# Encoder block on one core: last branch-B unit interleaved differently with the gate products, own staging pool for gate copies, token sums in halves, meta columns on VectorE

## The chip, the cores and the metric

The kernel runs on one core of a Trainium2 chip. Its engines are TensorE (PE; weight loads are listed as PEld), VectorE (DVE), ScalarE (ACT), GpSimd (POOL) and SyncE (SP), each with its own in-order queue. SP only starts transfers; ACT can start them too, on a queue of its own. The metric is the device time of one execution in microseconds (us).

## What is computed

One encoder block of width 1024 over 1024 tokens and 16 meta tokens, in float32. Two attention branches run on the same normed input, each with its gate, and a SwiGLU feed-forward network follows.

```python
def diff_attn_rows(q1, q2, k1, k2, v, qpos, kpos, key_real, slopes, lam):
    ...
    s1 = jnp.einsum('bqhd,bkhd->bhqk', q1, k1).astype(jnp.float32) * scale + bias
    s2 = jnp.einsum('bqhd,bkhd->bhqk', q2, k2).astype(jnp.float32) * scale + bias
    attn = jax.nn.softmax(s1, axis=-1) - lam * jax.nn.softmax(s2, axis=-1)
    return jnp.einsum('bhqk,bkhe->bqhe', attn.astype(v.dtype), v)

def mixer_block(h, w_in, ...):
    proj = h @ w_in
    ...
    y_a = differential_attention(...)
    y_b = windowed_gqa(...)
    merged = jax.nn.sigmoid(ga) * (y_a @ w_ba) + jax.nn.sigmoid(gb) * (y_b @ w_bb)
    return merged @ w_o

h = h + mixer_block(rms_norm(h, norm_mix[layer]), w_in[layer], ...)
h = h + swiglu(rms_norm(h, norm_ffn[layer]), w_ff_gate[layer], w_ff_up[layer], w_ff_down[layer])
return rms_norm(h, norm_final)[:, N_META:]
```

## The kernel before, in words

Float32 products are made of split operands: a high part and a low remainder, each product of two such operands taking three matmuls. The stages follow one another: norm and transposes, projections, branch B, branch A together with the gate projections, the merge of the branches (ppa), the output projection (po), and the feed-forward network (pg at L1699, pd at L1803). This change touches the end of branch B and branch A.

Branch B has 16 units (group g, token tile t), made by `attend_b`. A unit makes scores, an exp and a scaling; its `finish` then transposes each block on PE (T; L453, L439 for the meta block bmd), splits the result on ACT and DVE into btr (btm for the meta block), and multiplies by the values (V; L450, L459) into bpy. For the last unit (1,7) the steps are named T0, V0 for the meta block, T1, V1 for block 6 and T2, V2 for block 7 in this text; the code's list `last_unit` has them in that order, and in the change's table "V0" is the meta block's V, "T1" block 6 and so on. The unit's sum by1 is built by an ACT copy and a DVE add (L462) and stored to yb_d (L464).

Branch A has 32 tiles (head h, token tile t). In a tile `scores_a` makes two score maps m = 1 and m = 0 (aps, L1035), each with a 704-wide DVE operation (L1038) and a 336-wide one (L1042, which reads a copied distance strip far_m made by POOL at L982), an exp on ACT (L1046), and then the combination of the two maps on DVE (L1052) into as0_0 or as0_1 by turns. A meta copy (L1053) repeats 2 x 16 meta columns behind the combined map. Transposes (L1064), products with the values (L1077) and a norm follow. The psum bank pair "two" that the 704-wide operation reads has a single buffer.

The gate projections are computed by a scheme of products of block sums; `order_g` lists pairs (k, p), here called quarters. One quarter is 12 matmuls (pg, L928) on the split normed input hT_hi, hT_lo and an operand wopg that POOL makes from weights (cast L830, difference L831, sums L811 and L812) loaded by SP (L790). Results leave through ACT or DVE to staging tiles (L934, L948, L959, L964, L966) and are stored by SP (`flush_stores`, L892). `turn_into` (L860) loads sums of token halves t_d over parts of hT.

The order on PE is written out by hand: the strings SLOTS say for each tile which piece comes next, s scores, g four gate products, t transposes, n later steps. The order on POOL is written out at the head of branch A only. On the other engines a scheduler sets the order from its simulated times; `queue_behind` and `issue_after` are the places where the program sets an order between two instructions. Tiles of pools that share an address wait for the earlier user.

## Time and profile before

| what | value |
|---|---|
| median of three runs | 1423.49 us (1421.62 to 1425.19) |
| profiled execution | 1422.3 us, of which span 1420.5 us |
| mean granted TensorE clock | 0.997 |
| branch A begins (first aps) | at 280.49 us |
| last value product of branch A begins | at 596.46 us |

In the profile a row of the timeline gives the start, the duration, the engine, the line, the operation with output and inputs, how many stand in a row, and in brackets how long the engine stood idle before and what ended that. "Granted clock" is the share of full speed at which PE was let run. A row of the waits has the waiting group, what it waited for, and the total, the count and the longest wait.

### The profile page before, as it was taken

To read this page: it belongs to the slowest core of one execution; us is meant where nothing else is said; L and a number is where in the kernel's file an instruction comes from. 1 tells how busy PE (TensorE), PEld (TensorE's weight loads), DVE (VectorE), ACT (ScalarE), POOL (GpSimd) and SP (SyncE) were. 2 spreads that over 40 slices of the span, in tenths; PEclk is the share of its full clock that TensorE was granted. 3 is DMA by queue.
4 is the path that set the end of the run, shared out by engine and by line. 5 is a ranking of instruction groups with operands and counts; after the bars stand their busy time and mean duration, and the time that the engine had idled before them with its cause. 6 is when DMAs were issued, how large, how long until landed. Compare 5 with 4: busy or idle time off the path is not lost.

```text
span 1420.5 us, 20697 instructions
## 1 busy us (share of the span) xinstructions
PE 1400.6 (99%) x7171; PEld 1201.6 (85%) x7171; DVE 920.5 (65%) x1587; ACT 674.6 (47%) x1285; POOL 657.9 (46%) x666
## 2 busy tenths in 40 slices
PE   9999999899999999999999999999999999999998
PEld 8989999778888888878888888888888888888886
DVE  6546666656677777666978956544544453787566
ACT  6356565534444555555346644333333333444454
POOL 4156884366777767622503054554444441000442
PEclk9999999999999999999999999999999999999999
DMA  8446658543796453296422724432233223954333
GB/s 233 92 124 187 190 176 295 150 158 104 258 336 208 142 187 120 82 332 202 148 104 90 207 91 147 149 106 98 100 112 104 97 97 108 361 184 144 121 127 142
DMA packets 192952, 227.73 MB, mean 160 GB/s; under 512 B 16888, under 2 KB 126400, under 8 KB 192720
## 3 DMA queue, kind: packets, MB, share of 16 engines
q1 hardware_dynamic: 190656, 223.46, 48.3%
q10 hardware_dynamic: 2192, 2.96, 0.7%
q8 instruction: 56, 0.92, 0.3%
q14 instruction: 48, 0.39, 0.1%
HBM read 152.48 MB, written 68.39 MB: 155 GB/s over the span
## 4 chain that ended last, share of the span: by engine, by line
PE 73%; DVE 2%; POOL 1%; DMA 1%; issue 1%; ACT 1%; SPq 0%; DVEq 0%; POOLq 0%; ACTq 0%
PE pg L1699 29%; PE pd L1803 15%; PE pg L928 8%; PE ppa L746 6%; PE po L1602 4%; PE aps L1035 3%; PE apy L1077 3%; PE apt L1064 2%; PE po L1610 2%; DVE as L1052 1%; ACT as L1046 1%; POOL wopg L831 1%; DMA g_d<-g 1%; PE ptn_f L1567 0%; DVE as L1038 0%
## 5 line engine op out<-in xcount | busy, mean ns | idle before, releaser
L1699 PE MATMUL pg<-t,wop 128*128 128x512 f32 x1056 | 242.4, 389 | 0.0
L1699 PEld LDWEIGHTS pg<-t,wop 128*128 128x128 f32 x1056 | 198.2, 188 | 41.2
L121 POOL TENSOR_TENSOR wop<-wf,wop 128x512 fp32r<-128x512 f32 x114 | 150.7, 1323 | 164.3 <-ACT wop L120 152.5
L1803 PE MATMUL pd<-ob,oa 128*128 128x512 f32 x924 | 209.6, 389 | 0.0
L1803 PEld LDWEIGHTS pd<-ob,oa 128*128 128x128 f32 x924 | 173.4, 188 | 36.0
L928 PE MATMUL pg<-hT_hi,wopg 128*128 128x512 f32 x488 | 185.2, 405 | 7.0 <-ACT p L934 2.1
L1699 PE MATMUL pg<-b,wop 128*128 128x512 f32 x792 | 183.3, 389 | 0.0
L1699 PEld LDWEIGHTS pg<-b,wop 128*128 128x128 f32 x792 | 148.4, 188 | 30.7
L1046 ACT ACTIVATE as<-as,amn 128x1040 f32<-128x1040 f32 x64 | 74.7, 1166 | 97.7 <-DVE amn L1042 96.2
L120 ACT ACTIVATE wop<-wf 128x512 fp32r<-128x512 f32 x128 | 80.8, 632 | 72.3 <-PE pg L1699 50.9
L928 PEld LDWEIGHTS pg<-hT_hi,wopg 128*128 128x128 f32 x488 | 92.4, 190 | 24.6 <-POOL wopg L831 3.5
L121 POOL TENSOR_TENSOR oa<-ra,oa 128x512 fp32r<-128x512 f32 x27 | 34.9, 1294 | 168.6 <-ACT oa L120 167.2
L120 ACT ACTIVATE oa<-ra 128x512 fp32r<-128x512 f32 x77 | 48.7, 632 | 108.5 <-PE pd L1803 50.1
L928 PE MATMUL pg<-hT_lo,wopg 128*128 128x512 f32 x244 | 96.5, 396 | 0.0
L1035 PE MATMUL aps<-ak,aq 128*128 128x352 f32 (+1 forms) x384 | 87.5, 336 | 1.2 <-DVE amn L1038 1.2
L1476 DVE TENSOR_TENSOR s<-wf,wf 128x512 f32<-128x512 f32 x22 | 15.6, 709 | 111.6 <-DMA wf<-in_w_ff_up_dram 71.6
L1038 DVE CUSTOM_DVE_ANT_0 as<-aps,dist,far_a 128x704 f32<-128x704 f32 x64 | 60.4, 944 | 24.7 <-PE aps L1035 24.5
L1035 PEld LDWEIGHTS aps<-ak,aq 128*128 128x128 f32 x384 | 64.2, 191 | 9.8 <-DVE amn L1038 3.2
L414 DVE CUSTOM_DVE_ANT_0 bs<-bps,tbx,nsink 128x432 f32<-128x432 f32 (+1 forms) x64 | 38.5, 628 | 45.6 <-PE bps L412 31.8
L424 POOL TENSOR_SCALAR bs<-bs,bdn 128x432 f32<-128x432 f32 (+1 forms) x64 | 36.9, 597 | 51.1 <-DVE bdn L422 31.7
L1067 ACT ACTIVATE at<-apt 128x512 fp32r<-128x512 f32 (+1 forms) x96 | 46.3, 487 | 25.8 <-PE apt L1064 25.5
L1726 ACT COPY p<-pg 128x512 f32<-128x512 f32 x44 | 25.8, 587 | 66.6 <-PE pg L1699 66.6
(340 smaller groups left out, 3144.5 us busy)
## 6 DMA issues: line engine op xcount, KB each, us to landing
ra<-aop SPq DMA_DIRECT2D x77, 256.0 KB, 2.6
wf<-in_w_ff_gate_dram SPq DMA_DIRECT2D x25, 512.0 KB, 3.6
wf<-in_w_ff_up_dram SPq DMA_DIRECT2D x25, 512.0 KB, 3.7
aop<-as SPq DMA_DIRECT2D x44, 256.0 KB, 2.1
wg_s<-in_w_in_dram SPq DMA_DIRECT2D x18, 512.0 KB, 5.0
aop<-c SPq DMA_DIRECT2D x33, 256.0 KB, 2.0
ak<-ka_d SPq DMA_DIRECT2D x16, 520.0 KB, 7.0
t_d<-tst SPq DMA_DIRECT2D x16, 512.0 KB, 4.3
```

Source lines behind the costliest of these rows:

```text
L120: high = nc.scalar.activation(hi, src, AF.Copy)
L121: lo_eng.tensor_tensor(lo, src, f32(hi), ALU.subtract)
L746: nc.tensor.matmul(ps, w[:, a, j, :], src(j, b, tk), start=(j == 0 and n == 0), stop=(j == 3 and n == 2))
L928: product = nc.tensor.matmul(ps, op[:, x, c, :], h[:, 4 * d + c, HALF[t]], start=(p in (1, 6, 7) and c == 0 and i == 0), stop=(p in (2, 6, ...
L1035: nc.tensor.matmul(ps[:, :n], qs[m][:, t * P:(t + 1) * P], ks[m][:, vv, k0:k0 + n], start=(vv == 0), stop=(vv == 1))
L1038: nc.vector.tensor_tensor_reduce(s[m][:, 0:2 * n].rearrange("p (a k) -> p a k", a=2), two[:, :, :n], dist[:, u0:u0 + 2 * n].rearrange("p ( ...
L1046: nc.scalar.activation(s[m][:, 0:L], s[m][:, 0:L], AF.Exp, bias=mn[:, m, 1:2], scale=-1.0, accum_out=dn[:, 1:2] if m else first_sum)
L1067: nc.scalar.activation(hi, pt[:kp, :nb], AF.Copy)
L1077: nc.tensor.matmul(py[:, cols], v[:kp, a, k, :], at_[:kp, k, b, :], start=(k == 0 and j == 0), stop=(k == 8))
L1602: nc.tensor.matmul(sets_o[p][u], oa[:, a, u * P:(u + 1) * P], ob[:, b, :], start=(p in (1, 5) and j == 0 and k == 0), stop=(p in (2, 3) an ...
L1699: nc.tensor.matmul(ps, op[:, x, c, :], b[:, y, c, :], start=(p in (1, 5) and c == 0 and n == 0), stop=(p in (4, 2, 3) and c == 3 and n == ...
L1803: nc.tensor.matmul(ps[u], oa[:, a, u * P:(u + 1) * P], ob[:, b, :], start=(p in (1, 2, 5) and j == 0 and k == 0), stop=(p in (2, 3, 4) and ...
```

## The change

The change has six parts. The last unit of branch B is woven with the products of gate quarter (1,1) by a table, LAST_B. The staging tiles u and yg get a pool of their own, ustage. The strips far_m0 and far_m1 come first in the pool of branch A, so they lie elsewhere, and the memsets of as0 stand behind the operand of the sixth quarter. The token sums 0 and 2 are loaded in halves, and the loads of weights after the fourth are put behind the sums. Two yb_d stores and two gate stores (g3_6, g3_7) are started by ACT. The meta copy runs on DVE. The number of products, and the feed-forward part, are the same.

Line numbers in the changed kernel are higher: L450 becomes L453, L453 L456, L459 L462, L462 L465, L464 L467; L790 becomes L795, L830 and L831 become L835 and L836, L860 L865, L892 L900, L928 L937, L934 L944, L982 L999, L985 L1002, L1035 L1049, L1038 L1052, L1046 L1060, L1053 L1070; L1203 and L1206 become L1226 and L1229.

On PE, at the end of branch B, before (bpy_1_6 and bpy_1_7 are the sums of the last two units, bpt the transposed blocks, bmd1 the meta block's source, pg_1_1 the gate bank of quarter (1,1)):

```order
L928 MATMUL pg_1_1_3500<-hT_hi_139,wopg_1_1_3471 128x512 x2
L928 MATMUL pg_1_1_3500<-hT_lo_140,wopg_1_1_3471 128x512
L928 MATMUL pg_1_1_3500<-hT_hi_139,wopg_1_1_3471 128x512
L459 MATMUL bpy_1_6_2425<-btr_1_6_6_2450,vb1_154 128x512 x2
L459 MATMUL bpy_1_6_2425<-btr_1_6_7_2460,vb1_154 128x512 x2
L439 MATMUL bpt_1_7_8_2470<-ident_111,bmd1_156 128x128
L453 MATMUL bpt_1_7_6_2479<-ident_111,bs_1_7_2392 128x128 x4
L450 MATMUL bpy_1_7_2469<-btm1_158,vb1_154 128x512
L459 MATMUL bpy_1_7_2469<-btr_1_7_6_2484,vb1_154 128x512
L453 MATMUL bpt_1_7_7_2489<-ident_111,bs_1_7_2392 128x128 x4
L459 MATMUL bpy_1_7_2469<-btr_1_7_6_2484,vb1_154 128x512
L459 MATMUL bpy_1_7_2469<-btr_1_7_7_2494,vb1_154 128x512 x2
```

Twelve pg products stand ahead of the sixth and seventh blocks of unit (1,6), and the last unit runs without a break. The changed order there:

```order
L442 MATMUL bpt_1_7_8_2470<-ident_111,bmd1_156 128x128
L456 MATMUL bpt_1_7_6_2479<-ident_111,bs_1_7_2392 128x128 x4
L937 MATMUL pg_1_1_3504<-hT_hi_139,wopg_1_1_3473 128x512
L937 MATMUL pg_1_1_3504<-hT_lo_140,wopg_1_1_3473 128x512
L937 MATMUL pg_1_1_3504<-hT_hi_139,wopg_1_1_3473 128x512 x2
L937 MATMUL pg_1_1_3504<-hT_lo_140,wopg_1_1_3473 128x512
L937 MATMUL pg_1_1_3504<-hT_hi_139,wopg_1_1_3473 128x512
L453 MATMUL bpy_1_7_2469<-btm1_158,vb1_154 128x512
L456 MATMUL bpt_1_7_7_2489<-ident_111,bs_1_7_2392 128x128 x4
L937 MATMUL pg_1_1_3504<-hT_hi_139,wopg_1_1_3473 128x512
L937 MATMUL pg_1_1_3504<-hT_lo_140,wopg_1_1_3473 128x512
L937 MATMUL pg_1_1_3504<-hT_hi_139,wopg_1_1_3473 128x512 x2
```

Six pg products now stand between the transposes of block 6 and the meta product V0, and six between the transposes of block 7 and the products of blocks 6 and 7, which follow these rows.

On POOL, at the head of branch A, before (far_m is the distance strip, wg_f the raw weights, DMAHW names the completion of a transfer):

```order
L985 MEMSET far_m0_3429 128x16 [waits DMAHW4_49,DMAHW2_49,DMAHW6_49,DMAHW1_49,DMAHW7_49,DMAHW0_49,DVE_49]
L982 COPY far_m0_3429<-dist_852 128x320
L985 MEMSET far_m1_3430 128x16
L982 COPY far_m1_3430<-dist_852 128x320
L985 MEMSET far_m2_3431 128x16 [waits PE_49,Pool_49]
L990 MEMSET as0_0_3437 128x80 [waits PE_49,Activation_49]
L990 MEMSET as0_1_3438 128x80 [waits PE_49,Activation_49]
L982 COPY far_m2_3431<-dist_852 128x320
L830 CAST wopg_2_1_3531<-wg_f2_0_3464 128x512 [waits DMAHW2_49]
```

The first memset waits for six transfers and DVE, and the operand wopg_2_1 stands behind it. After:

```order
L1002 MEMSET far_m0_3431 128x16
L999 COPY far_m0_3431<-dist_852 128x320
L1002 MEMSET far_m1_3432 128x16
L999 COPY far_m1_3432<-dist_852 128x320
L1002 MEMSET far_m2_3433 128x16 [waits PE_49,Pool_49]
L999 COPY far_m2_3433<-dist_852 128x320
L835 CAST wopg_2_1_3522<-wg_f2_0_3466 128x512 [waits DMAHW0_49]
L836 TENSOR_TENSOR wopg_2_1_3522<-wg_f2_0_3466,wopg_2_1_3522 128x512 [waits Pool_49]
L816 TENSOR_TENSOR wg_f2_1_3468<-wg_f2_1_3468 128x512 [waits DMAHW1_49]
L817 TENSOR_TENSOR wg_f2_1_3468<-wg_f2_1_3468,wg_f2_0_3466 128x512 [waits Pool_49]
L835 CAST wopg_2_6_3527<-wg_f2_1_3468 128x512 [waits PE_49,Pool_49]
L836 TENSOR_TENSOR wopg_2_6_3527<-wg_f2_1_3468,wopg_2_6_3527 128x512 [waits Pool_49]
```

The first memset waits for nothing, and the waits for transfers are now with wg_f2 and, right behind the last row shown, with the memset of as0_0. On DVE, the first operation that writes as0_0 waits for a transfer in both kernels; as0_0 lies over the source of the last yb_d store in both.

On ACT, at the same place, before (p1 are the gate copies, by1 the branch-B sums):

```order
L443 ACTIVATE bmh_1_7_2472<-bpt_1_7_8_2470,columns_161 128x128 [waits DVE_49,PE_49,Activation_49]
L462 COPY by1_1_6_2465<-bpy_1_6_2425 64x512 [waits DMAHW6_49]
L456 ACTIVATE btr_1_7_6_2484<-bpt_1_7_6_2479 128x512 [waits PE_49]
L456 ACTIVATE btr_1_7_7_2494<-bpt_1_7_7_2489 128x512 [waits DVE_49,PE_49]
L462 COPY by1_1_7_2499<-bpy_1_7_2469 64x512 [waits DMAHW1_49,PE_49]
L464 DMA yb_d1_110<-by1_1_7_2499 64x4x128 [waits DVE_49]
L934 COPY p1_0_3495<-pg_0_1_3482 128x512
L934 COPY p1_1_3513<-pg_1_1_3500 128x512 [waits DMAHW6_49,DMAHW7_49,DMAHW5_49,DMAHW3_49]
L1046 ACTIVATE as1_0_0_3522,adn_0_0_3519<-as1_0_0_3522,amn_0_0_3518 128x1040 [waits DVE_49,Activation_49]
```

The copies p1_0 and p1_1 stand behind the store of unit (1,7). After:

```order
L944 COPY p1_0_3497<-pg_0_1_3484 128x512 [waits DMAHW6_49,DMAHW5_49,DMAHW7_49,DMAHW3_49,Activation_49]
L446 ACTIVATE bmh_1_7_2472<-bpt_1_7_8_2470,columns_161 128x128 [waits DVE_49,PE_49,Activation_49]
L465 COPY by1_1_6_2465<-bpy_1_6_2425 64x512
L459 ACTIVATE btr_1_7_6_2484<-bpt_1_7_6_2479 128x512 [waits PE_49]
L467 DMA yb_d1_110<-by1_1_6_2465 64x4x128 [waits DVE_49]
L459 ACTIVATE btr_1_7_7_2494<-bpt_1_7_7_2489 128x512 [waits PE_49,Activation_49]
L944 COPY p1_1_3517<-pg_1_1_3504 128x512 [waits DMAHW2_49,PE_49,Activation_49]
L465 COPY by1_1_7_2499<-bpy_1_7_2469 64x512 [waits DMAHW1_49,PE_49]
L467 DMA yb_d1_110<-by1_1_7_2499 64x4x128 [waits DVE_49]
L1060 ACTIVATE as1_0_0_3538,adn_0_0_3535<-as1_0_0_3538,amn_0_0_3534 128x1040 [waits DVE_49,Activation_49]
```

Both copies now stand ahead of it, and the store of unit (1,6) is among ACT's instructions.

On SP, at the end of branch A, before (g_d holds the gates, m0 and m1 are the operand blocks of the merge):

```order
L892 DMA g_d13_89<-g22_6_6782 128x512 [waits DMAHW4_49,DVE_49]
L892 DMA g_d12_88<-g3_6_6871 128x512 [waits DMAHW5_49,Activation_49]
L1203 DMA m0_6902<-in_w_branch_b_dram 128x4x128 [waits DMAHW6_49,PE_49]
L1203 DMA m0_6902<-in_w_branch_b_dram 128x4x128 [waits DMAHW7_49]
L1206 DMA m1_6903<-yb_d0_109 128x512 [waits DMAHW0_49,PE_49]
L1206 DMA m1_6903<-yb_d0_109 128x512 [waits DMAHW1_49]
```

After:

```order
L900 DMA g_d13_89<-g22_6_6790 128x512 [waits DMAHW0_49,DVE_49]
L1226 DMA m0_6910<-in_w_branch_b_dram 128x4x128 [waits DMAHW2_49,PE_49]
L1226 DMA m0_6910<-in_w_branch_b_dram 128x4x128 [waits DMAHW3_49]
L1229 DMA m1_6911<-yb_d0_109 128x512 [waits DMAHW4_49,PE_49]
L1229 DMA m1_6911<-yb_d0_109 128x512 [waits DMAHW5_49]
L1229 DMA m1_6911<-yb_d0_109 128x512 [waits DMAHW6_49]
```

The store g_d12 is gone from between; it is started by ACT. The wg_f2 loads stand ahead of wg_f3 at the head of branch A. Of the 32 meta copies, 16 stand on DVE ahead of the next tile's 704-wide operation and 16 behind it.

```diff
@@ constants
+N_PRE = 6
+ON_ACT = (1, 6), (1, 7)
+LAST_B = ("T1", 4), (5, "V0"), (5, "T2"), ("T2", 6), (7, "V1"), (7, "V2")
@@ attend_b, finish
-            queue = nc.scalar if (g, t) == (BG - 1, NT - 1) else nc.sync
-            queue.dma_start(yb_d[g][:, t * P:(t + 1) * P].rearrange("(r d) t -> d r t", r=4),
-                            y1.rearrange("d (r t) -> d r t", r=4))
+            queue = nc.scalar if (g, t) in ON_ACT else nc.sync
+            stores_b.append(queue.dma_start(yb_d[g][:, t * P:(t + 1) * P].rearrange("(r d) t -> d r t", r=4),
+                                            y1.rearrange("d (r t) -> d r t", r=4)))
@@ pools of branch A
     close_stage()
+    ustage, close_ustage = pool("ustage", "right")
     gstage, close_stage = pool("gstage", "right")
@@ load_g
                 if n_loaded[0] > 4:
                     after.enter_context(tc.issue_after(keys_a[0].ins))
+                    after.enter_context(tc.issue_after(raws_g[3].ins))
@@ turn_into
-        for c in (range(4) if i == 1 else (slice(0, 4),)):
+        for c in (range(4) if i == 1 else (slice(0, 2), slice(2, 4)) if i in (0, 2) else (slice(0, 4),)):
...
         turned_t[i] = last
+        if i == 2:
+            for late in raws_g[4:]:
+                queue_behind([late], last)
@@ gate_steps
         def kept_g(name):
-            return gstage.tile([P, 512], F32, tag="u", name=name, bufs=4)
+            return ustage.tile([P, 512], F32, tag="u", name=name, bufs=4)
...
-                with tc.issue_after(values_in[0].ins):
+                with tc.issue_after(values_in[0].ins), tc.issue_after(raws_g[3].ins):
...
-                        store(st, 2 * k + (p == 4), int(p == 3))
+                        if p == 3 and k > 5:
+                            nc.scalar.dma_start(g_d[2 * k][:, HALF[1]], st)
+                        else:
+                            store(st, 2 * k + (p == 4), int(p == 3))
...
-                quarters.append(product)
+                quarters.append((firsts[0], product))
@@ far_m, as0
+    far_m = [(gstage if i > 1 else apool).tile([P, 336], F32, name=f"far_m{i}") for i in range(3)]
+    apool.tile([P, 32], F32, name="apool_pad")
     apool.tile([P, 9, 2, 256], F32R, tag="at", name="at_room", bufs=AT_BUFS)
-    far_m = [(gstage if i > 1 else apool).tile([P, 336], F32, name=f"far_m{i}") for i in range(3)]
...
     s0s = [apool.tile([P, 9 * P], F32, name=f"as0_{i}") for i in range(2)]
-    for i in range(2):
-        nc.gpsimd.memset(s0s[i][:, L + 2 * NM:], 0.0)
@@ scores_a
-        nc.gpsimd.tensor_copy(s[0][:, L:L + 2 * NM].rearrange("p (a k) -> p a k", a=2),
-                              s[0][:, S:L].unsqueeze(1).broadcast_to([P, 2, NM]))
+        with ExitStack() as after:
+            if (h, t) == (0, 0):
+                after.enter_context(tc.issue_after(made_g[min(5, len(made_g) - 1)].ins))
+            nc.vector.tensor_copy(s[0][:, L:L + 2 * NM].rearrange("p (a k) -> p a k", a=2),
+                                  s[0][:, S:L].unsqueeze(1).broadcast_to([P, 2, NM]))
@@ normed_a
-        yg = gstage.tile([P, 512], F32, tag="yg", name=f"yg_{nm}", bufs=2)
+        yg = ustage.tile([P, 512], F32, tag="yg", name=f"yg_{nm}", bufs=2)
@@ head of branch A
                 if not h:
-                    for i, steps in enumerate(last_unit):
-                        queue_behind(steps, quarters[(1, 3, 3, 5, 5, 7)[i]])
+                    ensure_g(N_PRE)
+                    with tc.issue_after(made_g[min(5, len(made_g) - 1)].ins):
+                        for i in range(2):
+                            nc.gpsimd.memset(s0s[i][:, L + 2 * NM:], 0.0)
+                if not h:
+                    for after, late in LAST_B:
+                        behind = quarters[after][1] if isinstance(after, int) else last_unit["TV".index(after[0]) + 2 * int(after[1])][-1]
+                        queue_behind([quarters[late][0]] if isinstance(late, int) else last_unit["TV".index(late[0]) + 2 * int(late[1])], behind)
```

More of the change, by code (lines that the diff above doesn't have):

```diff
@@ L365, in encoder_block @@
     scaled = []
-    last_unit, quarters, sums_b = [], [], []
+    last_unit, quarters, sums_b, stores_b = [], [], [], []
     def queue_behind(late, first):
@@ L926, in gate_steps @@
             for c in range(4):
+                firsts = []
                 for i, (x, h) in enumerate(((0, hT_hi), (0, hT_lo), (1, hT_hi))):
@@ L930, in gate_steps @@
                                      stop=(p in (2, 6, 3, 4) and c == 3 and i == 2), skip_group_check=True)
+                    firsts.append(product)
                 if c == 3:
@@ L972, in gate_steps @@
                         del kept[k]
-                quarters.append(product)
+                quarters.append((firsts[0], product))
                 yield
             ensure_g(n + 4)
+    far_m = [(gstage if i > 1 else apool).tile([P, 336], F32, name=f"far_m{i}") for i in range(3)]
+    apool.tile([P, 32], F32, name="apool_pad")
     apool.tile([P, 9, 2, 256], F32R, tag="at", name="at_room", bufs=AT_BUFS)
-    far_m = [(gstage if i > 1 else apool).tile([P, 336], F32, name=f"far_m{i}") for i in range(3)]
     def far_copy(n):
         if n < AH * NT:
-            nc.gpsimd.tensor_copy(far_m[n % 3][:, 0:S - 704], dist[:, 1600 - n % NT * P:1600 - n % NT * P + S - 704])
+            with ExitStack() as after:
+                if n == 3:
+                    after.enter_context(tc.issue_after(made_g[min(5, len(made_g) - 1)].ins))
+                nc.gpsimd.tensor_copy(far_m[n % 3][:, 0:S - 704], dist[:, 1600 - n % NT * P:1600 - n % NT * P + S - 704])
     for i in range(3):
@@ L1052, in scores_a @@
         nc.vector.scalar_tensor_tensor(s[0][:, 0:L], s[1][:, 0:L], dn[:, 0:1], s[0][:, 0:L], ALU.mult, ALU.add)
-        nc.gpsimd.tensor_copy(s[0][:, L:L + 2 * NM].rearrange("p (a k) -> p a k", a=2),
-                              s[0][:, S:L].unsqueeze(1).broadcast_to([P, 2, NM]))
+        with ExitStack() as after:
+            if (h, t) == (0, 0):
+                after.enter_context(tc.issue_after(made_g[min(5, len(made_g) - 1)].ins))
+            nc.vector.tensor_copy(s[0][:, L:L + 2 * NM].rearrange("p (a k) -> p a k", a=2),
+                                  s[0][:, S:L].unsqueeze(1).broadcast_to([P, 2, NM]))
     def transpose_a(h, t, s, at_):
@@ L1238, in encoder_block @@
     close_stage()
+    close_ustage()
     close_wpool()
```

## The prediction

> **What bounds the kernel now.** I read the page's first part, then its costliest groups, then the waits of the matrix engine (PE), then the timeline at the two places where those waits stand.
>
> ```profile
> span 1420.5 us, 20697 instructions
> PE 1400.6 (99%) x7171; PEld 1201.6 (85%) x7171; DVE 920.5 (65%) x1587; ACT 674.6 (47%) x1285; POOL 657.9 (46%) x666
> L1038 DVE CUSTOM_DVE_ANT_0 as<-aps,dist,far_a 128x704 f32<-128x704 f32 x64 | 60.4, 944 | 24.7 <-PE aps L1035 24.5
> ```
>
> PE is busy for 99% of the span, and the change removes no product. So it can gain only where PE waits, or where PE is busy at a lower clock: the 19.9 us outside its busy time, plus stretched products. Two of the waits at the head of branch A (262 to 330 us), in total, times and longest:
>
> ```profile
> PE pg L928 <- ACT p L934: 2.1, 1, 2.1
> PE pg L928 <- POOL wopg L831: 0.6, 1, 0.6
> ```
>
> The timeline of PE gives their places and those of two more, and the table of windows the granted clock (third from the right, 0.66):
>
> ```profile
> 271.22 0.62 PE L459 MATMUL bpy<-btr,vb 128*128 128x512 f32 x2
> 271.67 0.39 PE L928 MATMUL pg<-hT_hi,wopg 128*128 128x512 f32 x1
> 274.42 1.08 PE L459 MATMUL bpy<-btr,vb 128*128 128x512 f32 x4
> 277.58 0.50 PE L450 MATMUL bpy<-btm,vb 128*128 128x512 f32 x1 [1.53 <-DVE btm L446]
> 280.16 0.50 PE L459 MATMUL bpy<-btr,vb 128*128 128x512 f32 x1 [0.22 <-DVE btr L457]
> 280.49 0.80 PE L1035 MATMUL aps<-ak,aq 128*128 128x352 f32 x4
> 283.38 0.79 PE L928 MATMUL pg<-hT_hi,wopg 128*128 128x512 f32 x1 [2.08 <-ACT p L934]
> 283.97 0.63 PE L928 MATMUL pg<-hT_lo,wopg 128*128 128x512 f32 x1
> 290.07 0.39 PE L928 MATMUL pg<-hT_hi,wopg 128*128 128x512 f32 x1
> 294.19 0.80 PE L1035 MATMUL aps<-ak,aq 128*128 128x352 f32 x4
> 298.69 0.50 PE L928 MATMUL pg<-hT_hi,wopg 128*128 128x512 f32 x1 [1.31 <-POOL wopg L830]
> 300.74 0.90 PE L1035 MATMUL aps<-ak,aq 128*128 128x352 f32 x4
> 280.00:290.00 10.00, 7.76 (x25) 6.43 (x26) 1.65 (x4) 1.66 (x3) 0.00 (x0) 0.66 1.01 331
> ```
>
> Between 280 and 290 us the granted clock averages 0.66, so PE is at half speed for about two thirds of it (a gate product is 0.63 long at 283.97, 0.39 at 290.07). Other engines stand still there, and this shows why:
>
> ```profile
> 282.02 0.68 ACTq L464 DMA_DIRECT2D yb_d<-by  x1
> 282.74 1.07 ACT L934 COPY p<-pg 128x512 f32<-128x512 f32 x2 [1.46 <-DVE by L462]
> 290.30 0.11 POOL L985 MEMSET far_m<- 128x16 f32 x1 [16.13 <-issue]
> 290.83 0.57 DVE L1042 CUSTOM_DVE_ANT_0 as<-aps,far_m,amn 128x336 f32<-128x336 f32 x1 [7.97 <-POOL far_m L982]
> ```
>
> The last store of branch B leaves ACT's queue at 282.02. POOL's memset of far_m0, which lies over that store's source and waits for it, starts at 290.30: the store lands at most 8.28 us after its issue. Behind the memset stand the gate operands (the 1.31 and 0.62 us waits) and the first 336-wide score operation of VectorE (DVE). Behind the store in ACT's own order stand the p copies (the 2.08 us wait).
>
> **The change, part by part.**
>
> A, the head. The two waits of the last unit go: half of quarter (1,1) stands behind T1, while DVE makes btm, and half behind T2. From 271.22 to 280.49 is 9.27 us; less 1.53 and 0.22 it is 7.52, with the same products, so the first aps starts at 278.75. The cover is those 12 products, 2.75 us from 271.67 to 274.42 before (0.23 each); without it 1.53 comes back. Then p1_0 is copied before the unit's end and nothing waits for it: what began at 281.30 (283.38 less the wait) begins at 279.56. From 283.38 to 290.07 stand 12 gate and 8 score products. At 0.23 and some 0.16 (the 0.80 of four at 294.19 less the overlap of the last) they are 4.05 us where the half clock took 6.69, so 279.56 + 4.05 = 283.6 stands for 290.07. Another 12 gate products and 3 more (0.23 each) bring PE to tile 1's first scores at 287.0.
>
> Here something is late that was hidden before. Tile 0's second score tile, as0_0, still lies over the source of the last store, and its 704-wide DVE operation waits for that store; tile 1's scores need the bank that this operation reads. In the row of before the store is issued 1.53 after the first aps (282.02 against 280.49), so now at 280.28. On SP's queue wg_f2 and the token sums stand ahead of it, the same bytes as before, the sums in pieces of 512 KB:
>
> ```profile
> hT_hi<-t_d SPq DMA_DIRECT2D x1, 1024.0 KB, 8.6
> hT_lo<-t_d SPq DMA_DIRECT2D x1, 1024.0 KB, 10.4
> yb_d<-by SPq DMA_DIRECT2D x2, 128.0 KB, 2.4
> 292.91 0.95 DVE L1038 CUSTOM_DVE_ANT_0 as<-aps,dist,far_a 128x704 f32<-128x704 f32 x1
> 297.73 0.94 DVE L1038 CUSTOM_DVE_ANT_0 as<-aps,dist,far_a 128x704 f32<-128x704 f32 x1
> ```
>
> A 128 KB store lands after 2.4 us when little is in flight, behind megabytes after up to 8.28. The same megabytes are in flight, so I take the far end: 280.28 + 8.28 = 288.56. From as0_0's 704 operation (292.91) to the end of tile 1's first (297.73 + 0.94 = 298.67) is 5.76 us of DVE, ACT and DVE. With the meta copy between (0.21), tile 1's second scores, at 300.74 before, start at 288.56 + 5.97 = 294.53: a gain of 6.2. PE's own work would bring them at 291.2 (9.5, the end for a store that lands in 2.4). If the store lands no earlier than before, at 290.30, they start at 296.27: 4.5. I take 6.2. PE's stall at 287.0 lasts until 288.56 + 0.95, so 2.5 us. POOL no longer waits for the store ahead of wopg but for wg_f2, which SP now loads ahead of the sums; that hides in the stall.
>
> B, 32 meta copies leave POOL. D, they come to DVE.
>
> ```profile
> L1053 POOL COPY as<-as 128x32 f32<-128x32 f32 x32 | 6.7, 209 | 23.0 <-DVE as L1052 17.1 <-PE apt L1064 2.1 <-PE apy L1077 1.3
> PE pg L928 <- POOL wopg L831: 0.9, 3, 0.4
> L268 DVE COPY vt_va<-vt_va x4: 177/334/551, 127.4 to 242.8; 128x16 f32<-128x16 f32 x4
> 305.41 2.43 DVE L1052 SCALAR_TENSOR_TENSOR as<-as,adn,as 128x1040 f32<-128x1040 f32 x1
> L1052 DVE SCALAR_TENSOR_TENSOR as<-as,adn,as 128x1040 f32<-128x1040 f32 x32 | 47.0, 1470 | 0.8
> ```
>
> On POOL a copy takes 0.21, but the queue stood 17.1 us in front of it, waiting for DVE's result, with the operands of the gates behind. From 310 to 600 us PE waited 0.9 us for them, in three waits. I take −0.9, ends 0 and −0.9. On DVE nothing of its kind is measured; the nearest row is a copy of half the width: 0.18 to 0.55. Of the 32, 16 stand ahead of the next 704 operation, 16 behind it. Before the 704 operations DVE sat 24.5 us idle waiting for PE, over 64 of them, against 16 x 0.21 = 3.4. I take +0.3, for the few tiles in which it was not idle. The ends are 0 and, were all 32 at 0.55 on PE's path, +17.6.
>
> By the Trainium skill, "SBUF — State Buffer", section "Who interferes with whom", a DVE copy can take the port pair shared with GpSimd (POOL) as a lock, and the second instruction fully blocks. The row at 305.41 agrees that the two engines collide: 2.43 us against a mean of 1.47. By that rule the copies would come at the long end, which is the slower rival below.
>
> C, the end of branch A.
>
> ```profile
> 597.27 0.32 SPq L892 DMA_DIRECT2D g_d<-g  x1
> 597.68 1.00 SPq L1203 DMA_DIRECT2D m<-in_w_branch_b_dram  x2
> 598.78 4.25 SPq L1206 DMA_DIRECT2D m<-yb_d  x8
> 610.33 0.69 DVE L121 TENSOR_TENSOR yb<-m,yb 128x512 fp32r<-128x512 f32 x1 [1.11 <-ACT yb L120]
> 610.94 0.68 DVE L959 TENSOR_TENSOR g<-pg,q 128x512 f32<-128x512 f32 x1
> 611.77 0.47 PE L928 MATMUL pg<-hT_hi,wopg 128*128 128x512 f32 x1 [1.66 <-DVE g L959]
> 612.08 0.39 PE L928 MATMUL pg<-hT_lo,wopg 128*128 128x512 f32 x1
> 596.46 0.99 PE L1077 MATMUL apy<-at,av 128*128 128x256 f32 x7
> ```
>
> PE waits 1.66 us for a gate sum that stands on DVE behind a split of yb, which waits for a load of m1. The loads stand on SP behind the store of g_d12, issued at 597.27 once ACT's copy was ready. That store goes to ACT's queue now, so the two weight loads go earlier and the eight yb loads once their space is free (the last apy, 597.45) instead of 598.78: 1.3 us sooner. The DMA issue costs ACT a slot of about 0.7 (its row at 282.02), which hides as ACT is busy for 47% of the span. I take −1.3, with ends 0 and −1.66: the wait is all there is.
>
> The sum: −6.2 − 0.9 + 0.3 − 1.3 = −8.1. The profiled execution took 1422.3 (its span and 1.8 around it), so 1414.2. It lies 1.2 below the median 1423.5; on the median's basis I predict 1415.4.
>
> **The rivals.** *The clock halves again* in the new 2.5 us stall. For it: it halved before among waits of 1.53, 0.22 and 2.08. Against: after 1.66 us at 611.77 the next product is at full pace (0.39). 2.5 lies above both, but nothing else waits in that window. The half clock cost 6.69 − 4.05 = 2.65 before; with it again the head gains 3.6, the sum is −5.5, the time 1418.0.
>
> By the Trainium skill, "TensorE: Matmul & The Clock Gate", section "What's actually happening", the clock drops after at least one idle window of about 3.4 us; by it this rival could not happen. Here it dropped with no single wait over 2.08, so the trace does not bear the rule out as it stands, and I leave the rival a large chance.
>
> *The change doesn't do what it says, since transfers bind*: the store lands at 290.30 as before, because the same bytes are ahead of it, and the loads of yb at 598.78 are bound by transfer, not issue. Head −4.5, end 0: −4.5 − 0.9 + 0.3 = −5.1, or 1418.4. For it speaks the DMA share of 1.01 in the windows row; against it, that SP starts both sets of loads earlier too.
>
> *Slower*: the copies on DVE and POOL's casts lock each other out and lengthen DVE's path in every tile. Place: ahead of the 704 operations and, on POOL, the gate operands. The rest gives −8.4, so it decides from 8.4 + 4.3 = 12.7 us, 0.40 a copy on PE's path in all 32 tiles. At the longest row, 0.55, it is +17.6: 1423.5 + 9.2 = 1432.7. Against it: the idle 24.5 us, and the 16 copies behind the 704 operations.
>
> **How the numbers follow.** A difference of 0.3% (4.3 us) is about what a measurement of this kernel can tell from no change, so faster ends at 1419.2. Chances: forecast 0.42; clock again 0.32; transfers bind 0.12; both of these 0.06 (near 1421); slower 0.08. The forecast's own range runs from −9.5 − 0.9 − 1.66 = −12.1 to −4.5 − 0.9 + 0.3 = −5.1: 1411.4 to 1418.4. The whole range takes in the rivals on the fast side and, at the low end, the 1.9 us by which a run of before lies under its median: 1409.5 to 1421. Faster holds the forecast, three quarters of the clock case and two thirds of the transfer case: 0.74. Same holds the rest of these and both together: 0.18. Slower 0.08.
>
> **What would show it.** Right: no wait of bpy on btm; the first aps about 278.8; POOL's far_m memset with no wait before it; as0_0's 704 operation waiting for the yb store until about 288.6, with PE idle some 2.5 us; a granted clock near 1.00 from 280 to 300; tile 1's second scores near 294.5; meta copies on DVE of about 0.2; the wait on the gate sum at the end of branch A near 0.4; from there on the same durations, some 8 us earlier. Wrong: a clock under 0.8 from 288 to 296; a store that lands after 290, or so early that PE never waits; meta copies over 0.4, with more than a few tenths of PE waiting on DVE's amn; the loads of yb not earlier against the last apy.

## The result

| kernel | median, us | runs | ratio to before, 95% interval |
|---|---|---|---|
| before | 1422.45 (1421.27 to 1425.19) | 9 | |
| changed | 1418.86 (1417.66 to 1419.73) | 9 | 0.9973 [0.9963, 0.9984] |

The change gains 3.6 us, 0.27%, where 8.1 us were forecast. The time lies in the stated range, but 3.5 us above the forecast, and just inside what the prediction called faster (below 1419.2). The range reaches to 1421 and so speaks little for the sum. By the medians 4.5 us of the gain are missing; the time is off by less because the median of before, 1423.49 in the three runs that the forecast was built on, is 1422.45 in nine. The profiled execution has a span of 1415.9 us against 1420.5, so 4.6 us less.

The profile of the changed kernel, first part:

```profile
span 1415.9 us, 20684 instructions
PE 1398.6 (99%) x7171; PEld 1199.3 (85%) x7171; DVE 939.8 (66%) x1619; ACT 674.0 (48%) x1285; POOL 667.0 (47%) x634
```

PE's waits in it from 262 to 620 us (total, times, longest):

```profile
PE aps L1049 <- DVE amn L1052: 3.9, 6, 1.6
PE apt L1081 <- DVE at L1085: 1.3, 1, 1.3
PE pg L937 <- POOL wopg L836: 0.6, 1, 0.6
PE apt L1081 <- DVE amn L1056: 0.4, 1, 0.4
```

The waits on ACT's p copy, on btm and on the gate sum at the end of branch A are gone, and of the wopg waits 0.6 is left. In their place stands one name: DVE, with 5.6 us. Before, the waits on DVE's amn were 1.2 us in this stretch.

The head in the timeline of the changed kernel:

```profile
277.58 0.81 PE L1049 MATMUL aps<-ak,aq 128*128 128x352 f32 x4
279.12 0.58 ACTq L467 DMA_DIRECT2D yb_d<-by  x1
286.40 0.95 DVE L1052 CUSTOM_DVE_ANT_0 as<-aps,dist,far_a 128x704 f32<-128x704 f32 x1 [5.70 <-DMA yb_d<-by]
287.41 0.91 PE L1049 MATMUL aps<-ak,aq 128*128 128x352 f32 x4 [1.61 <-DVE amn L1052]
292.64 0.92 PE L1049 MATMUL aps<-ak,aq 128*128 128x352 f32 x4 [0.42 <-DVE amn L1052]
301.58 0.66 PE L1081 MATMUL apt<-ident,as 128*128 128x128 f32 x4 [1.34 <-DVE at L1085]
302.64 0.92 PE L1049 MATMUL aps<-ak,aq 128*128 128x352 f32 x4 [0.40 <-DVE amn L1052]
553.74 0.91 PE L1049 MATMUL aps<-ak,aq 128*128 128x352 f32 x4 [0.93 <-DVE amn L1052]
```

And one row of the table of windows:

```profile
280.00:290.00 10.00, 8.39 (x41) 6.93 (x40) 2.70 (x9) 3.57 (x6) 6.96 (x10) 1.00 0.97 314
```

The store leaves ACT at 279.12, and DVE's first operation on as0_0 starts when it has landed, 7.28 us later. PE waits 1.61 us for it. The clock stays at 1.00 (third column from the right). Behind the stall stand three more waits on DVE, of 0.42, 1.34 and 0.40, and late in branch A one of 0.93.

PE runs the same 7171 products in nearly the same order in both kernels, so the two traces can be laid side by side product by product. The lead of the changed kernel over the kernel before, in the profiled executions:

| at (us, before) | what | lead, us | gained in this stretch |
|---|---|---|---|
| 265 | end of the stages that the change does not touch | 0.95 | 0.95 |
| 300.7 | second scores of tile 1 | 8.09 | 7.1 |
| 332 | third and fourth tile | 6.70 | −1.4 |
| 535 | | 6.94 | 0.2 |
| 609 | just ahead of the last gate wait | 4.15 | −2.8 |
| 645 | merge | 5.73 | 1.6 |
| 1216 | start of the last products pd | 4.66 | −1.0 |

The 0.95 at the start comes up between 45 and 55 us, in code that is the same. At 265 us the profiled executions of the kernels here lie between 2.2 us behind the kernel before and 1.1 us ahead of it, so it is no effect of the change. The last row is a wait of 0.7 us of pd on DVE's ob, which other executions have at 0.2, 0.4 or not at all.

So the head gave more than forecast, and branch A gave 4 us back: 1.4 right behind the head and 2.8 late.

### The profile page after: what moved, and what is told of

Read it like the earlier page. It is cut to its first block, busy times and chain, and to the rows that moved or that the text cites. A ratio compares the mean times of both kernels' runs of the same rounds, so it can differ in the third digit from the quotient of the medians.

```text
span 1415.9 us, 20684 instructions
## 1 busy us (share of the span) xinstructions
PE 1398.6 (99%) x7171; PEld 1199.3 (85%) x7171; DVE 939.8 (66%) x1619; ACT 674.0 (48%) x1285; POOL 667.0 (47%) x634
## 4 chain that ended last, share of the span: by engine, by line
PE 90%; DVE 4%; ACT 2%; issue 1%; DMA 1%; POOL 1%; SPq 0%; DVEq 0%; ACTq 0%; POOLq 0%
PE pg L1723 29%; PE pd L1827 14%; PE pg L937 8%; PE ppa L749 6%; PE po L1626 4%; PE pp_va L235 3%; PE pp_ka L235 3%; PE pp_qb L235 3%; PE aps L1049 3%; PE apy L1094 3%; PE bps L415 2%; PE pp_qa L235 2%; PE po L1634 2%; PE apt L1081 2%; PE bpy L462 1%
## 5 line engine op out<-in xcount | busy, mean ns | idle before, releaser
L124 POOL TENSOR_TENSOR wop<-wf,wop 128x512 fp32r<-128x512 f32 x114 | 154.1, 1353 | 162.3 <-ACT wop L123 150.5
L937 PE MATMUL pg<-hT_hi,wopg 128*128 128x512 f32 x488 | 183.1, 401 | 0.7 <-POOL wopg L836 0.6
L1060 ACT ACTIVATE as<-as,amn 128x1040 f32<-128x1040 f32 x64 | 74.6, 1165 | 105.2 <-DVE amn L1056 99.7
L937 PEld LDWEIGHTS pg<-hT_hi,wopg 128*128 128x128 f32 x488 | 91.7, 188 | 15.4 <-POOL wopg L836 1.1
L937 PE MATMUL pg<-hT_lo,wopg 128*128 128x512 f32 x244 | 96.0, 393 | 0.0
L1049 PE MATMUL aps<-ak,aq 128*128 128x352 f32 (+1 forms) x384 | 87.4, 336 | 4.5 <-DVE amn L1052 3.9
L1049 PEld LDWEIGHTS aps<-ak,aq 128*128 128x128 f32 x384 | 63.0, 189 | 15.1 <-DVE amn L1052 9.0
L1052 DVE CUSTOM_DVE_ANT_0 as<-aps,dist,far_a 128x704 f32<-128x704 f32 x64 | 60.3, 942 | 21.8 <-PE aps L1049 15.9
L1094 PEld LDWEIGHTS apy<-at,av 128*128 128x128 f32 x400 | 54.1, 189 | 4.1
```

The source lines that it names most:

```text
L124: lo_eng.tensor_tensor(lo, src, f32(hi), ALU.subtract)
L937: product = nc.tensor.matmul(ps, op[:, x, c, :], h[:, 4 * d + c, HALF[t]], start=(p in (1, 6, 7) and c == 0 and i == 0), stop=(p in (2, 6, ...
L1049: nc.tensor.matmul(ps[:, :n], qs[m][:, t * P:(t + 1) * P], ks[m][:, vv, k0:k0 + n], start=(vv == 0), stop=(vv == 1))
L1052: nc.vector.tensor_tensor_reduce(s[m][:, 0:2 * n].rearrange("p (a k) -> p a k", a=2), two[:, :, :n], dist[:, u0:u0 + 2 * n].rearrange("p ( ...
L1060: nc.scalar.activation(s[m][:, 0:L], s[m][:, 0:L], AF.Exp, bias=mn[:, m, 1:2], scale=-1.0, accum_out=dn[:, 1:2] if m else first_sum)
L1094: nc.tensor.matmul(py[:, cols], v[:kp, a, k, :], at_[:kp, k, b, :], start=(k == 0 and j == 0), stop=(k == 8))
```

## Experiments

Line numbers in the rows are those of each kernel.

### Addresses alone

On the kernel before, only where tiles lie:

```diff
+    far_m = [(gstage if i > 1 else apool).tile([P, 336], F32, name=f"far_m{i}") for i in range(3)]
+    apool.tile([P, 160], F32, name="apool_pad")
     apool.tile([P, 9, 2, 256], F32R, tag="at", name="at_room", bufs=AT_BUFS)
-    far_m = [(gstage if i > 1 else apool).tile([P, 336], F32, name=f"far_m{i}") for i in range(3)]
```

> The kernel before with only addresses changed: far_m0, far_m1 and a pad of 640 bytes first in branch A's pool, so that neither far_m nor as0 lies over the sources of the last stores. PE's order is that of before. Theory: the waits for the store were the larger part of the head's loss; the two waits on wopg (1.9 us) go and with them DVE's wait of 8 us, while 1.53, 0.22 and 2.08 stay: 2 to 5 us faster than before, with the low end if the clock halves again. Rival: without the new order on PE and ACT the gate operands are late for wg_f2's load, and less than 1.5 us is gained.

Measured: 1417.34 us (1416.21 to 1417.55), ratio 0.9963 [0.9951, 0.9976]: 4.9 us faster than before, where the whole change gave 3.6; the intervals overlap, so it is as much, and not shown to be more. In the trace 5.0 are gained from 265 to 320 us, and 1.0 at the end of branch A, where PE waits 0.6 in place of 1.66. Its waits from 262 to 330 us:

```profile
PE pg L928 <- ACT p L934: 2.1, 1, 2.1
PE bpy L450 <- DVE btm L446: 1.5, 1, 1.5
PE bpy L459 <- DVE btr L457: 0.2, 1, 0.2
```

The two wopg waits (1.3 and 0.6) are gone and nothing has taken their place; the waits of the last unit and for the p copy stay, as the theory had it.

### as0_0 off the store's source, in the changed kernel

```diff
-    apool.tile([P, 32], F32, name="apool_pad")
+    apool.tile([P, 160], F32, name="apool_pad")
```

> The changed kernel with the pad in branch A's pool made 512 bytes larger, so that as0_0 no longer lies over the source of unit (1,7)'s store and its first DVE operation waits for PE alone. Theory: PE's stall of 1.6 us ahead of tile 1's first scores goes, and DVE's chain behind it starts 3 to 5 us earlier, so tile 1's second scores come 2 to 3 us sooner: about 1416.5 us. Rival: the next wait takes its place (the gate operand of quarter (2,6), behind wg_f2's load and POOL's sums, or the psum bank), and under 0.7 us is gained.

Measured: 1412.74 us (1412.38 to 1413.53), ratio 0.9936 [0.9923, 0.9948]: 6.1 us faster than the changed kernel by the medians, 5.3 by the spans of the profiled executions. That is over twice what the theory said. From 262 to 330 us PE waits for nothing but 0.2 us:

```profile
PE bpy L453 <- DVE btm L449: 0.2, 1, 0.2
```

Product by product it leads the changed kernel by 1.5 us at the stall, 2.5 at tile 1's second scores and 4.8 at 303 us. Before branch A it had been 0.35 behind. So the stall of 1.61 was worth about 5 us: DVE, which had stood idle for 5.70 us, stayed late for three more tiles, and PE met it again at 292.64, 301.58 and 302.64.

Lateness is not all of it. The wait of 1.34 at 301.58 stands behind a combination of the two maps that meets POOL's sum of weights. In the changed kernel:

```profile
298.50 2.43 DVE L1066 SCALAR_TENSOR_TENSOR as<-as,adn,as 128x1040 f32<-128x1040 f32 x1
298.53 1.30 POOL L816 TENSOR_TENSOR wg_f<-wg_f 128x512 f32<-128x512 f32 x1
```

With as0_0 apart:

```profile
294.73 1.30 DVE L1066 SCALAR_TENSOR_TENSOR as<-as,adn,as 128x1040 f32<-128x1040 f32 x1
294.83 2.36 POOL L816 TENSOR_TENSOR wg_f<-wg_f 128x512 f32<-128x512 f32 x1
```

The same two operations overlap in both, and one of them takes over 1 us longer: here DVE's, there POOL's. It goes with the stall: this second combination takes 2.4 us in all four executions that have the stall and 1.3 in the five of the changed order that do not. (In the kernel before it takes 2.43 too, but PE, later there, waits only 0.2 behind it.) Some 1.1 of the 5 us (an estimate, 2.43 less 1.30) are thus the collision, and not DVE's lateness as such.

### Meta copies on DVE alone

On the kernel before:

```diff
-        nc.gpsimd.tensor_copy(s[0][:, L:L + 2 * NM].rearrange("p (a k) -> p a k", a=2),
+        nc.vector.tensor_copy(s[0][:, L:L + 2 * NM].rearrange("p (a k) -> p a k", a=2),
```

> The kernel before with only the meta copies moved to DVE. Theory: 2 to 3.5 us slower than before, all of it between 300 and 610 us, copies of 0.17 to over 1 us. Rival: 0 to 0.9 us faster than before, since POOL's queue no longer waits for DVE's combination of the maps.

Measured: 1424.14 us (1423.39 to 1426.46), ratio 1.0016 [1.0007, 1.0025]: 1.9 us slower. Product by product 2.0 us are lost between 543 and 577 us, with these waits from 530 to 600 us (before had only 0.5 us of them there):

```profile
PE aps L1035 <- DVE amn L1038: 1.0, 1, 1.0
PE apt L1064 <- DVE amn L1042: 0.4, 1, 0.4
```

From 530 to 590 us it is 2.6; against it, 0.8 is gained from 310 to 500, and 1.0 at the end of branch A, where PE comes later and its wait on the gate sum falls from 1.66 to 1.0. The expected size, 2 to 3.5, was a little high; the place was narrower than expected.

### Meta copies back on POOL, in the changed kernel

The edit is the same line of the changed kernel with `nc.gpsimd` for `nc.vector`.

> The changed kernel with the 32 meta copies back on POOL. Theory: on DVE the copies hold each other up with POOL's casts (mean 0.48 us, up to 1.26, in the changed kernel), and this is where branch A from 305 to 610 us gave back 3 us; then this kernel keeps the head (second scores of tile 1 near 293) and gains 2 to 3.5 us in that stretch, about 1416 us. Rival: the stretch was lost to the new order of POOL and SP; then it stays as long as in the changed kernel, or grows by up to 0.9 us for the gate operands, 1419 to 1420 us.

Measured: 1418.59 us (1416.12 to 1420.13), ratio 0.997 [0.9961, 0.998]: no different from the changed kernel. In the trace, which is 3.2 us behind already at 265 us, in code that is the same, both theories act. From 314 us to the end of branch A it gains 3.2 us on the changed kernel, as the theory says; but at 305 to 314 it loses 2.9, with a wopg wait of 1.0 us and a granted clock of 0.83 from 300 to 310 us (half from about 305 to 309), which the profiled execution of the changed kernel does not have. So the price of the copies was there. What took it up again is the late gate operand (1.3 of the 2.9 us), which with copies on POOL comes without the stall too (a wait of 1.9 us, below), and the half clock (1.6). Whether the half clock comes in the other executions of this kernel no trace shows.

### The same two with as0_0 apart

POOL:

```diff
-    apool.tile([P, 32], F32, name="apool_pad")
+    apool.tile([P, 160], F32, name="apool_pad")
...
-            nc.vector.tensor_copy(s[0][:, L:L + 2 * NM].rearrange("p (a k) -> p a k", a=2),
+            nc.gpsimd.tensor_copy(s[0][:, L:L + 2 * NM].rearrange("p (a k) -> p a k", a=2),
```

> The changed kernel with as0_0 apart from the store's source and the meta copies on POOL. With no stall at the head that could hide or add to it, this shows the price of the copies on DVE. Theory (they hold each other up with POOL): 1.5 to 2.5 us faster than with the copies on DVE and as0_0 apart (1412.7), so about 1410.7. Rival: POOL's queue waits for DVE again, the gate operands are late by 0.5 to 1 us, and it comes out the same or slower.

Measured: 1411.44 us (1410.8 to 1412.94), ratio 0.9927 [0.9914, 0.9939]: 1.3 us faster than with the copies on DVE by the medians, with intervals that overlap. In the trace theory and rival both act: 2.4 us are gained from 500 to 577 us, and 2.2 are lost at 303 to 306, with a wait of 1.9 us for a gate operand:

```profile
PE pg L937 <- POOL wopg L836: 1.9, 1, 1.9
```

ACT, with the same pad:

```diff
-            nc.vector.tensor_copy(s[0][:, L:L + 2 * NM].rearrange("p (a k) -> p a k", a=2),
+            nc.scalar.copy(s[0][:, L:L + 2 * NM].rearrange("p (a k) -> p a k", a=2),
```

> The changed kernel with as0_0 apart and the meta copies on ACT, which is busy for half of the time and stands behind neither queue. Theory (the copies' price is the collision of DVE and POOL): 1.5 to 2.5 us faster than with them on DVE (1412.7), about 1410.7, copies of about 0.2 us. Rival: ACT's order holds the copy behind an exp or the exps behind the copy, waits of PE on DVE's amn or on the transposes grow, and nothing is gained.

Measured: 1409.10 us (1408.72 to 1409.55), ratio 0.9907 [0.9891, 0.9922]: 3.6 us faster than with the copies on DVE and 13.2 us faster than before. It is the fastest of all kernels here, called the best kernel below. In the trace 2.8 us are gained, from 530 to 577. Its waits from 262 to 620 us:

```profile
PE pg L937 <- POOL wopg L836: 0.6, 1, 0.6
PE aps L1049 <- DVE amn L1052: 0.3, 1, 0.3
```

The copies in the kernels, by source line (shortest, median and longest in ns), before on POOL, changed on DVE, the last kernel on ACT:

```profile
L1053 POOL COPY as<-as x32: 201/209/216, 297.9 to 590.5; 128x32 f32<-128x32 f32 x32
```

```profile
L1070 DVE COPY as<-as x32: 164/299/1261, 291.5 to 586.2; 128x32 f32<-128x32 f32 x32
```

```profile
L1070 ACT COPY as<-as x32: 210/218/231, 286.8 to 577.6; 128x32 f32<-128x32 f32 x32
```

On POOL and ACT the copies differ by 0.02 us at most. On DVE the shortest is the quickest of all, but the longest takes 1.26. The timeline of the changed kernel shows a long one, and POOL at the same time, and then a short one:

```profile
550.85 0.87 DVE L1085 TENSOR_TENSOR at<-apt,at 128x512 fp32r<-128x512 f32 x2
551.65 1.17 DVE L1070 COPY as<-as 128x32 f32<-128x32 f32 x1
552.74 0.93 DVE L1052 CUSTOM_DVE_ANT_0 as<-aps,dist,far_a 128x704 f32<-128x704 f32 x1
551.48 1.31 POOL L836 TENSOR_TENSOR wopg<-s1g,wopg 128x512 fp32r<-128x512 f32 x1
552.75 1.26 POOL L825 TENSOR_TENSOR wg_s<-wg_s,wg_s 128x512 f32<-128x512 f32 x1
318.67 0.17 DVE L1070 COPY as<-as 128x32 f32<-128x32 f32 x1
318.69 1.29 POOL L836 TENSOR_TENSOR wopg<-wg_f,wopg 128x512 fp32r<-128x512 f32 x1
```

The copy at 551.65 starts just after POOL's difference and ends as that ends; the next scores' reduction starts behind it at 552.74, and PE waits 0.93 for it at 553.74. By the Trainium skill, "SBUF — State Buffer", section "Who interferes with whom", a DVE instruction in a mode that uses two ports and one of GpSimd (POOL) shut each other out: the one that issues first has the shared ports for its whole instruction, and the other blocks. These rows agree, with 1.17 us for a copy that takes 0.16 at its shortest. So do the other copies of the changed kernel: 23 of the 32 start while POOL is in a 128x512 operation, and 22 of these end 0.03 to 0.04 us after it, however much of it was left. The other nine, of which the one at 318.67 starts 0.02 us ahead of POOL, take 0.16 to 0.18.

### ACT for the copies, with the stall

The same line on ACT in the changed kernel, without the larger pad.

> The changed kernel with only the meta copies on ACT; as0_0 still waits for the store. Theory: the copies' price and the stall add: as far below the changed kernel (1418.9) as with as0_0 apart, 2.7 to 3.6 us, about 1415.7. Rival: the stall's aftermath (the waits of 0.4 and 1.3 us behind it, and in some executions the half clock) is DVE's late chain, which the copies lengthen or not at will, and the gain is under 1.5, as it was with POOL.

Measured: 1416.03 us (1414.55 to 1417.45), ratio 0.9955 [0.9943, 0.9967]: 2.8 us below the changed kernel. On ACT the copies' price and the stall add, at the low end of the theory. Its profiled execution too has the clock low behind the stall (half from 304.0 to 307.4), which costs 1.6 us against the changed kernel, not made up by 400 us:

```profile
300.00:310.00 10.00, 8.24 (x36) 6.57 (x35) 7.60 (x15) 4.78 (x9) 6.10 (x7) 0.83 0.08 29
```

### Without the weave

In the changed kernel, and then in the best one, the last unit stands behind the gate products as before:

```diff
-                    for after, late in LAST_B:
-                        behind = quarters[after][1] if isinstance(after, int) else last_unit["TV".index(after[0]) + 2 * int(after[1])][-1]
-                        queue_behind([quarters[late][0]] if isinstance(late, int) else last_unit["TV".index(late[0]) + 2 * int(late[1])], behind)
+                    for i, steps in enumerate(last_unit):
+                        queue_behind(steps, quarters[(1, 3, 3, 5, 5, 7)[i]][1])
```

> The changed kernel with the last branch-B unit put behind the gate products as before (no weave). Theory: the two waits come back (1.5 and 0.2 us), the first scores come some 1.7 us later, the store of unit (1,7) too, and with it everything that waits for it: 1.5 to 2 us slower than the changed kernel, about 1420.6. Rival: the 1.6 us wait for the store's landing takes them up, since transfers set it: within 0.5 us of the changed kernel.

Measured: 1421.29 us (1418.7 to 1423.19), ratio 0.9997 [0.9988, 1.0006]: 2.4 us slower than the changed kernel. In the trace it is 2.0 behind at the first scores. Behind the stall, here 2.04, the clock is at half from 290.9 to 294.2 (0.83 over 290 to 300 us); that puts it 4.0 behind at 291 us, but by 302 it is 2.5 again, where the wait on DVE's at is 0.83 instead of 1.34.

> The kernel with as0_0 apart and meta copies on ACT (1409.1), its last branch-B unit put behind the gate products as before. Both kernels have no wait for the store, so this prices the weave alone. Theory: the waits of 1.53 and 0.22 us come back and nothing behind them takes them up: 1.5 to 2 us slower, 1410.8. Rival: PE, coming earlier, only waits longer behind (for a gate operand or a bank), as the half clock was made up for in the end-store run: within 0.5 us.

Measured: 1412.1 us (1410.67 to 1417.29), ratio 0.9934 [0.992, 0.9949]: 3.0 us slower than the best kernel by the medians; in the trace it is 1.10 behind at 265 us and 3.24 behind at the first scores, so 2.1 belongs to the edit, with these waits:

```profile
PE bpy L453 <- DVE btm L449: 1.5, 1, 1.5
PE bpy L462 <- ACT btr L459: 0.2, 1, 0.2
PE bpy L462 <- DVE btr L460: 0.2, 1, 0.2
```

Nothing behind takes the waits up. What lies ahead of the edit is the part of the kernel in which executions differ anyway.

### The stores at the end of branch A

On the kernel before, the two stores alone:

```diff
-                        store(st, 2 * k + (p == 4), int(p == 3))
+                        if p == 3 and k > 5:
+                            nc.scalar.dma_start(g_d[2 * k][:, HALF[1]], st)
+                        else:
+                            store(st, 2 * k + (p == 4), int(p == 3))
```

> The kernel before with only the stores of g3_6 and g3_7 started by ACT. Theory: the loads of yb are issued about 1.3 us earlier, and PE's wait of 1.66 us on the gate sum at the end of branch A falls below 0.5: 1.2 to 1.7 us faster than before. Rival: the loads are bound by transfer; the wait stays above 1.2 and the time within 0.5 us of before.

Measured: 1420.55 us (1419.16 to 1422.5), ratio 0.9992 [0.9983, 1.0001]: 1.7 us by the medians, with an interval that just holds 1. At the end of branch A PE no longer waits, and leads the kernel before by 3.0 us there against 1.4 behind the head, of which 1.0 was there at 63 us: 1.6 us gained. This execution shows something else at the head, where its kernel is the same as before:

```profile
282.46 0.50 PE L928 MATMUL pg<-hT_hi,wopg 128*128 128x512 f32 x1 [2.08 <-ACT p L934]
292.02 0.47 PE L928 MATMUL pg<-hT_hi,wopg 128*128 128x512 f32 x1 [2.50 <-ACT g L948]
```

```profile
280.00:290.00 10.00, 7.44 (x35) 5.77 (x33) 2.07 (x5) 1.43 (x3) 1.05 (x7) 1.00 1.06 357
```

The clock stays at 1.00, PE is 3.5 us ahead at 290 us, 2.6 of it since 281 us, and then waits 2.50 for ACT's g copy, which stands behind an exp that waits, through DVE, for POOL's far_m. At 296 us the lead is 1.4, 0.4 more than at 281. So the half clock of the execution shown before cost next to nothing: PE would have waited there.

In the best kernel, the stores back on SP (the condition is never true):

```diff
-                        if p == 3 and k > 5:
+                        if p == 3 and k > 99:
```

> The kernel with as0_0 apart and meta copies on ACT (1409.1), with the stores of g3_6 and g3_7 back on SP. Theory: the 1.7 us that these stores gained alone on the kernel before are lost again: a wait of PE on the gate sum at the end of branch A of 1.2 to 1.7 us, 1410.6. Rival: other rows have moved there too (q_7 earlier, the store of ya later), and under 0.6 us is lost.

Measured: 1409.74 us (1409.11 to 1411.28), ratio 0.9913 [0.99, 0.9926]: 0.6 us slower than the best by the medians, with intervals that overlap, and 0.9 in the trace. The rival was nearer: the wait comes back at 0.7 us and a wait of 0.2 on ACT's q, not 1.66.

## Why the prediction was right and where it failed

**Right: the head's mechanism.** The waits on btm and on the p copy went, the first scores stand at 277.58, or 278.53 with the 0.95 that was there ahead of it (278.75 forecast), far_m waits for no transfer, and PE stalls at tile 1's first scores for the store under as0_0, as the second paragraph of part A said. The store took 7.28 us, not the 8.28 taken as the bound, so the stall was 1.61 and not 2.5, and the second scores of tile 1 gained 7.1 us and not 6.2.

**Failed: where part A stops.** The sum ended at tile 1's second scores, as if a gain that has got so far stays. It did not: DVE, idle for 5.70 us, stayed behind for three tiles, its second combination took 2.43 us beside POOL's sum of weights, as in the kernel before, but now PE stood waiting behind it (1.34 against 0.2), and PE gave back 1.4 us by 332. Moving as0_0 away shows the whole price of that stall: about 5 us, not the 3.3 that part A had between "landing at 8.28" (6.2) and "PE's own work" (9.5).

**Failed: part D, the meta copies.** It said +0.3, from a mean of 0.21 and 24.5 us of idle DVE time. They took 0.48 on the mean (15.4 us in 32), over the 0.4 that the prediction named as a sign of being wrong, and alone they cost 1.9 us; in the changed kernel the stretch from 535 to 609 gave back 2.8. The idle time was the wrong cover: it is a sum over 64 places, and the losses come in the few tiles where DVE is late and POOL is in the midst of a 1.3 us instruction. The upper end of the range for D (+17.6) and the rule named beside it had the right cause. Part B's −0.9 came to −0.3 (wopg waits of 0.9 before and 0.6 after from 310 us on). B and D together were forecast at −0.6. By the two runs with as0_0 apart, taking the copies off DVE is worth 1.3 us (to POOL, not clear of the noise) or 3.6 us (to ACT; 2.8 in the trace).

**Right: part C.** The yb loads are issued 1.3 us earlier against the same products (593.42, with a lead of 4.1 then, against 598.78), and the wait of 1.66 is gone: 1.6 gained, 1.3 forecast. In the best kernel the same stores are worth 0.6 (0.9 in the trace), not clear of the noise.

**The rivals.** The half clock did not come in the profiled execution of the changed kernel, with waits of 1.61, 0.42 and 1.34; it came in three others with the same stall (copies on POOL, copies on ACT, no weave), and in none of the five without it. Five of the nine executions of the changed kernel have a mean granted clock of 0.997, against 0.999 in the profiled one, so it may have come in these as well; no trace shows it. That the profiled one was spared is luck: its stall of 1.61 was longer than the 1.5 of one that was not. The price of 2.65 that the prediction gave to a half clock of 6.8 us was wrong where it was read: the end-store run shows that PE waits in its place. Behind the stall, 3.4 us at half clock cost 1.6 in two executions and nearly nothing in the third. That price stood in part A too, as the 6.69 − 4.05 of a stretch that was going to wait anyway; it did no harm there, since the chain through DVE set the end. "Transfers bind" was refuted at both places: the store has landed at 286.40 (287.35 with the 0.95) and not at 290.30, and the yb loads were issued earlier. The slower rival named the right cause and overstated it: the copies alone were 1.9 us slower, not 17.6.

The forecast of −8.1 thus failed by its size. The profiled executions differ by 4.6, so 3.5 are missing: 3.2 in D with B (2.6 lost from 332 to 609 us where 0.6 gained was forecast), 0.5 in part A (0.9 above the forecast up to tile 1, 1.4 given back behind it), and 1.0 at the start of pd in this one execution; against these, 0.3 more came in part C and 0.95 from the untouched stages at the start, which is chance and is not in the medians' 3.6.

## What to carry to other kernels

Before a new order is written, look for what a tile lies over: 512 bytes of pad were worth 6.1 us by the medians, and on the old kernel addresses alone gained as much as all parts of the change together. A stall of an engine that is not the bound can be paid more than once: here 1.6 us became 5, by the engine's lateness and by what it then ran into. Follow it until its slack has come back, not to the next milestone. Cover for an instruction on DVE is to be sought in each tile, with POOL's rows beside it, not in a sum of idle time; an engine whose copies show no spread beside the two, here ACT (0.210 to 0.231 us), is the better place even where its shortest copy is slower.

## What was not expected of the hardware

The clock halved in executions with waits of no more than 2.08 us, and stayed whole in one with waits of 2.08 and 2.50 within ten microseconds of each other, in the same code. The length of the waits alone does not tell it. In windows of 1 us, each stretch at half clock ahead of the last 10 us of a span was 3.4 us long (five executions) or 6.8 (the kernel before). By the Trainium skill, "TensorE: Matmul & The Clock Gate", section "What's actually happening", the window that decides runs freely, which would fit that the same code goes either way; that the clock drops after an idle window of about 3.4 us does not fit these rows, if an idle window is one without a product.

A DVE copy of 128x32 took from 0.164 to 1.261 us in one kernel, a spread of almost eight, while the same copy on POOL stayed within 0.201 to 0.216.
